# A twelfth pair: the last gate's second half of columns in seven products, and the final norm's products later

## The chip, the cores and the metric

The kernel runs on one core of one Trainium2 chip. The metric is the device time of one execution in microseconds (us), as the median of several runs. The profile and the trace come from one further execution, recorded by the hardware profiler. Engines are named as the profile names them: PE is TensorE (PEld its weight loads), DVE is VectorE, ACT is ScalarE, POOL is GpSimd, and SP issues most of the loads.

## The reference, cut to what matters

One layer of a hybrid decoder for 256 tokens of width 2048 in float32. The last two steps of it, and the norm behind them, are what the change touches:

```python
x = x + merged @ w_out
x = x + jax.nn.sigmoid(rmsnorm(x, ple_norm_g) @ w_pg) * (p_i @ w_pp)
return rmsnorm(x, final_norm_g)
```

`w_pg` is 2048 x 2048. Before that come one wide input projection (2048 x 13824), three branches (two kinds of attention and a gated recurrence), and their projections, which the change leaves alone.

## The kernel before, in words

**Products.** A float32 product is made of three matmuls: each operand is split into a high part of a shorter format (`fp32r`) and the rest, and `mm3` (lines 194 to 198) issues high x high, high x low and low x high into the same bank. Weights come as tiles of 128 x 1024: two k-tiles of 128 rows for 512 columns each (a chunk). `fetch` (line 112) loads one from SP's queue into one of six raw buffers; `split` casts the high part on ACT (line 141) and subtracts on DVE (line 147) into one of four pairs of buffers (`wsp`), or, for names in `kept`, into a block that stays. The 256 tokens are two halves of 128, and each half has its own bank of the matrix accumulators (`ps_mm`, two accumulators of two banks); four further banks (`ps_x`, the function `aux`) serve everything else.

**Pairs.** Two chunks of columns, a and b, can go together (`pair_of`, line 264). For the first four k-tiles (`PAIRED`) the work is seen as a 2 x 2 by 2 x 2 product: token halves by even and odd k-tiles, even and odd k-tiles by the two chunks. Eight block products become seven on sums and differences of the blocks. The activations' sums are made once (`make_sums`, line 248: five operations on DVE, a cast on ACT, a subtraction on DVE). The weights' sums are made in a chain tile: loads from SP, and adding loads from POOL's queue (`add_to`, line 275), each of which waits until the split before has read the tile. Products `seven`, `one`, `six` and `five` come ahead (`heads`) and leave partial results in two spare banks, which ACT and DVE move into the accumulators (`place`, line 281, and `on_vector`, line 277). Then `rest` runs the other twelve k-tiles of both chunks and sets `three`, `two` and `four` between them. Eleven pairs exist: nine in the input projection and two in the output projection.

**Order.** The program is traced as Python. A scheduler with a model of the engines then fixes each engine's order; `high_priority` moves an instruction ahead and `issue_after` ties one behind another. Every weight tile of `weights_of`, and some products of a pair, count as a tick (line 155): work given to `later(n, ...)` is put into the program n ticks on.

**The last stage.** The output projection's result is added to x (`residual`, line 1149), turned to feature-major through DRAM (`turn_later`, line 1066, on ACT's queue) and split into `x2T`. The gate (lines 1215 to 1259) has four chunks of 512 columns. Chunks 0 and 1 run their first twelve k-tiles each, then their last four; the last four need the part of x that is turned last. Chunk 2 follows whole. Chunk 3 is split for its end: first token half 0 with 512 columns, then token half 1 as two pieces of 256 columns, so that the final norm of the first half can run meanwhile; its weights stay in place (four blocks and the four split buffers). Behind each chunk, `output` (line 1181) makes the sigmoid on ACT, the product with the parked `p_i @ w_pp` (`pps`), the sum with x, and the squares for the final norm; the function that it returns multiplies by the final norm's weights `fg` (line 1188), and `gated` (line 1210) calls it at once. `pps` and `fg` are loaded on ACT's queue from two ticks after the output projection on (line 1174). At the end `store` scales by the norm and writes out.

Of the kernel before, what the change touches and what calls it, by code (L numbers as in the profile page):

```python
# [16 lines left out]
P = 128  # L17
D = 2048
SEQ = 256
NH = SEQ // P  # L20
BW = D // 2
KD = D // P
KB = BW // P
CW = 512
# [23 lines left out]
THEN = 2  # L48
SETTLE = 10
RV = 384  # L50
PAD = 256
# [3 lines left out]
def trunk(ctx: ExitStack, tc: tile.TileContext, x, early, table, onehot, maskv, w_in, sinks, conv, w_ri, vec, fin, w_br,  # L55
# [138 lines left out]
    def mm3(ps, a, b, first, last, **more):  # L194
        (ah, al), (bh, bl) = a, b
        nc.tensor.matmul(ps, ah, bh, start=first, stop=False, **more)  # L196
        nc.tensor.matmul(ps, ah, bl, start=False, stop=False, **more)  # L197
        nc.tensor.matmul(ps, al, bh, start=False, stop=last, **more)  # L198

# [63 lines left out]

    def pair_of(act, sums, src, row, name, inside=False, adds=4, early=1):
        names = ("11", "12", "22", "21")
# [28 lines left out]
        def product(n, a, r, dst, start=False, stop=False):  # L294
            w = split(f"{name}_m{n}", r, n == 1)
            for q in range(2):
                mm3(dst, a(q), [t[:, q * CW : (q + 1) * CW] for t in w], q == 0 and start, q == 1 and stop,
                    skip_group_check=True)

# [40 lines left out]
        def two():  # L340
            pss.append(matrix_psum(f"{name}_1"))
            for h in range(NH):
                place(pss[1][:, h], z[h])
            r = raw_of(3)
            with tc.issue_after(banks[1]):
                product(2, whole(1, 0), r, pss[1][:, 0])
                if adds < 4:
                    on_vector(chain, chain, r, ALU.add)

        def four():  # L350
            product(4, whole(1, 1), chain, pss[1][:, 1])
            tick()
# [5 lines left out]

        def rest(ends, done, at_turn=(0, 2, 4), then=None):
            while coming and coming[0] in heads:  # L360
# [14 lines left out]

            turns = [(i, k) for a, b in zip((PAIRED,) + ends, ends) for i in range(2) for k in range(a, b, WT // CW)]
            for n, (i, k) in enumerate(turns):
                head(len(turns) - n)
                usual(i, k)
                if n in at_turn:  # L380
                    (three, two, four)[at_turn.index(n)]()
                if k + WT // CW == KD:
                    done(i, pss[i])
                if then is not None and n == THEN:
                    then()

        t = block(f"b_{name}")
# [481 lines left out]

    def flip(dst, srcs, n, name, queue=nc.sync):  # L870

# [6 lines left out]
        for a in range(4):  # L878
            queue.dma_start(to[a], t[quad[a]].rearrange("i (b c) -> i b c", b=4))
        queue.dma_start(dst, d)  # L880

# [184 lines left out]
    def turn_later(u, n, src, name, gain=None, ticks=TURN_LATE):  # L1066
# [14 lines left out]
        later(ticks, finish)  # L1081
        if n == 0 and name == "m":
            later(ticks + 1, lambda: sums_of(u, name))

# [88 lines left out]
    for n, (to, src) in enumerate(rows):  # L1173
        later(2 + n, lambda to=to, src=src: nc.scalar.dma_start(to, src))
    HW = CW // 2
# [25 lines left out]
    def store(h, r, pieces):  # L1201
        for eng, c0, c1 in pieces:
# [5 lines left out]
            eng.dma_start(out[h * P : (h + 1) * P, c0:c1], sl)  # L1208

    def gated(n, ps):  # L1210
        y, junk = token_major(temp(f"y{n}")), token_major(temp(f"jz{n}"))
        for h in range(NH):
            output(h, n * CW, CW, ps[:, h, :], y[:, h, :], junk[:, h, :], square_act(h, n))()

    pss = [matrix_psum(f"pg{i}").rearrange("p h c -> p (h c)") for i in range(2)]
    gets = [weights_of(w_pg, i * KD * CW // WT, f"pg{i}", WT // CW) for i in range(2)]
    for last in (False, True):
        for i in range(2):
            for k in range(KD - 4, KD) if last else range(KD - 4):
                w, kk = gets[i](k)  # L1220
                c = slice(kk * CW, (kk + 1) * CW)
                for h in range(NH):
                    mm3(pss[i][:, h * CW : (h + 1) * CW], [t[:, h * P : (h + 1) * P] for t in act_of(*x2T)[k]],
                        [t[:, c] for t in w], k == 0, k == KD - 1)
            if last:
                gated(i, pss[i].rearrange("p (h c) -> p h c", h=NH))
    gated(2, project(act_of(*x2T), w_pg, 2 * KD * CW // WT, "pg2"))

    kept.update(f"pg3_{s}" for s in range(KD // 4))
# [6 lines left out]
    nc.gpsimd.tensor_tensor(rs3[:, :1], part[:, :1], half_c[:, :1], op=ALU.pow)  # L1236
    store(0, rs3[:, :1], ((nc.sync, 0, BW), (nc.scalar, BW + CW, D), (nc.sync, BW, BW + CW)))

    def part_of(c):
        def get(k):  # L1240
            w, kk = ws(k)
            return [t[:, kk * CW + c * HW : kk * CW + (c + 1) * HW] for t in w], 0
        return get
# [114 lines left out]
```

## Time and profile before

| what | us |
|---|---|
| median of 3 runs | 979.05 |
| lowest and highest of them | 978.0 and 981.14 |
| the profiled execution's own time | 977.16 |
| its span, first to last instruction | 975.1 |
| PE busy in the span | 965.5 |
| DVE busy | 721.8 |
| ACT busy | 620.9 |

The profiled execution is a little faster than the median, so a sum made on its rows is carried to the median by the difference. The granted clock of TensorE is 0.998. In the views, a line such as `L147 DVE TENSOR_TENSOR wl_pg<-r_pg,wh_pg` names the source line, the engine, the operation, and what is written from what. In order of time, the first number of a row is its start from the beginning of the span, the second its duration; in groups, busy time and the mean of one stand behind the bar; idle time ahead of an instruction and what ended it stand last.

### The profile page before, as it was taken

The page shows a single profiled execution, that of the slowest core. Times are in us where ns is not written, and L with a number is a line of the kernel's source. Part 1 is how long each engine was busy: PE and PEld are TensorE (multiplying, and loading weights), DVE is VectorE, ACT ScalarE, POOL GpSimd, SP SyncE. Part 2 cuts the span into 40 slices and gives each one's busy share as a digit, 9 for nine tenths or more (in the row PEclk, how much of TensorE's full clock was granted, in tenths as well). Part 3 has the DMA queues.
Part 4 walks back from the last instruction along what each step waited for, and adds up shares of the span by engine and source line. Part 5 has one row for each costly group of instructions (what it writes and reads, how often), then busy time and mean ns, then how long its engine had stood idle before and what let it go on. Part 6 is the DMA issues. An engine that isn't in the chain of part 4 may idle for free.

```text
span 975.1 us, 12612 instructions
## 1 busy us (share of the span) xinstructions
PE 965.5 (99%) x4390; PEld 804.3 (82%) x4390; DVE 721.8 (74%) x1005; ACT 620.9 (64%) x881; POOL 33.1 (3%) x45
## 2 busy tenths in 40 slices
PE   9999999999999999999999999999999999999996
PEld 7888888888888888888888888888888888888886
DVE  6855898866897676667677788788578587765673
ACT  7654776667777666556566866765566565665652
POOL 0010000010000000000000000000000000000000
PEclk9999999999999999999999999999999999999999
DMA  9978989799989865897787876776978998788742
GB/s 342 352 236 253 328 270 340 249 308 281 305 266 321 257 219 189 249 280 244 237 282 245 286 230 225 231 227 208 303 203 280 301 297 305 254 278 334 233 151 87
DMA packets 90264, 255.71 MB, mean 262 GB/s; under 512 B 10152, under 2 KB 31704, under 8 KB 90072
## 3 DMA queue, kind: packets, MB, share of 16 engines
q1 hardware_dynamic: 72720, 216.69, 64.4%
q0 software_dynamic: 4752, 17.30, 9.8%
q10 hardware_dynamic: 12728, 20.91, 6.4%
q8 instruction: 34, 0.56, 0.2%
q14 instruction: 30, 0.25, 0.1%
HBM read 234.13 MB, written 20.75 MB: 261 GB/s over the span
## 4 chain that ended last, share of the span: by engine, by line
PE 98%; DMA 0%; DVE 0%; ACT 0%; SPq 0%; issue 0%; DVEq 0%; ACTq 0%
PE ps_in L197 21%; PE ps_in L196 20%; PE ps_in L198 20%; PE ps_pg L198 3%; PE ps_pg L196 3%; PE ps_pg L197 3%; PE ps_out L196 3%; PE ps_out L198 3%; PE ps_out L197 3%; PE ps_bra L197 1%; PE ps_bra L196 1%; PE ps_brc L197 1%; PE ps_brc L198 1%; PE ps_brc L196 1%; PE ps_brb L197 1%; PE ps_brb L196 1%
## 5 line engine op out<-in xcount | busy, mean ns | idle before, releaser
L147 DVE TENSOR_TENSOR wl_in<-r_in,wh_in 128x1024 fp32r<-128x1024 f32 x196 | 239.0, 1222 | 95.6 <-ACT wh_in L141 91.3
L197 PE MATMUL ps_in<-wl_in,h 128*128 128x512 f32 x784 | 305.6, 390 | 0.4 <-DVE wl_in L147 0.4
L196 PE MATMUL ps_in<-wh_in,h 128*128 128x512 f32 x784 | 305.6, 390 | 0.0
L198 PE MATMUL ps_in<-wh_in,h 128*128 128x512 f32 x784 | 305.3, 389 | 0.0
L141 ACT CAST wh_in<-r_in 128x1024 fp32r<-128x1024 f32 x196 | 205.3, 1051 | 141.3 <-PE ps_in L198 105.1
L197 PEld LDWEIGHTS ps_in<-wl_in,h 128*128 128x128 f32 x784 | 147.3, 188 | 30.4 <-DVE wl_in L147 0.8
L198 PEld LDWEIGHTS ps_in<-wh_in,h 128*128 128x128 f32 x784 | 147.2, 188 | 30.4
L196 PEld LDWEIGHTS ps_in<-wh_in,h 128*128 128x128 f32 x784 | 147.2, 188 | 30.0
L147 DVE TENSOR_TENSOR wl_in_m<-b_in,wh_in_m 128x1024 fp32r<-128x1024 f32 x36 | 43.9, 1220 | 22.7 <-ACT wh_in_m L141 22.2
L147 DVE TENSOR_TENSOR wl_pg<-r_pg,wh_pg 128x1024 fp32r<-128x1024 f32 x28 | 33.9, 1222 | 27.4 <-ACT wh_pg L141 26.6
L141 ACT CAST wh_in_m<-b_in 128x1024 fp32r<-128x1024 f32 x36 | 37.8, 1049 | 25.0 <-PE ps_in L198 13.1
L275 POOL DMA_DIRECT2D b_in<-w_in_dram x29 | 25.5, 878 | 638.6 <-DMA b_in<-w_in_dram 395.7
L196 PE MATMUL ps_pg<-wh_pg,x_hi 128*128 128x512 f32 (+1 forms) x120 | 45.0, 375 | 0.0
L197 PE MATMUL ps_pg<-wl_pg,x_hi 128*128 128x512 f32 (+1 forms) x120 | 45.0, 375 | 0.0
L198 PE MATMUL ps_pg<-wh_pg,x_lo 128*128 128x512 f32 (+1 forms) x120 | 45.0, 375 | 0.0
L141 ACT CAST wh_pg<-r_pg 128x1024 fp32r<-128x1024 f32 x28 | 29.1, 1049 | 22.1 <-PE ps_pg L198 17.3
L196 PE MATMUL ps_out<-wh_out,m_hi 128*128 128x512 f32 x96 | 37.3, 389 | 0.0
L197 PE MATMUL ps_out<-wl_out,m_hi 128*128 128x512 f32 x96 | 37.3, 389 | 0.0
L198 PE MATMUL ps_out<-wh_out,m_lo 128*128 128x512 f32 x96 | 37.3, 389 | 0.0
L147 DVE TENSOR_TENSOR wl_out<-r_out,wh_out 128x1024 fp32r<-128x1024 f32 x24 | 29.1, 1220 | 10.2 <-ACT wh_out L141 10.2
L141 ACT CAST wh_out<-r_out 128x1024 fp32r<-128x1024 f32 x24 | 25.2, 1050 | 12.5 <-PE ps_out L198 8.1
L141 ACT CAST wh_brb<-r_brb 128x1024 fp32r<-128x1024 f32 x16 | 16.9, 1053 | 20.6 <-PE ps_brb L198 10.9
(360 smaller groups left out, 1638.3 us busy)
## 6 DMA issues: line engine op xcount, KB each, us to landing
r_in<-w_in_dram SPq DMA_DIRECT2D x223, 512.0 KB, 4.9
r_pg<-w_pg_dram SPq DMA_DIRECT2D x32, 512.0 KB, 4.8
r_out<-w_out_dram SPq DMA_DIRECT2D x30, 512.0 KB, 5.0
b_in<-w_in_dram POOLq DMA_DIRECT2D x29, 512.0 KB, 8.4
b_in<-w_in_dram SPq DMA_DIRECT2D x18, 512.0 KB, 5.3
r_brc<-w_br_dram SPq DMA_DIRECT2D x16, 512.0 KB, 6.3
r_bra<-w_br_dram SPq DMA_DIRECT2D x16, 512.0 KB, 4.3
r_brb<-w_br_dram SPq DMA_DIRECT2D x16, 512.0 KB, 6.3
```

Source lines behind the costliest of these rows:

```text
L141: casts.append(nc.scalar.copy(hi[:, c], r[:, c]).ins)
L147: los.append(nc.vector.tensor_tensor(lo[:, c], r[:, c], of, op=ALU.subtract).ins)
L196: nc.tensor.matmul(ps, ah, bh, start=first, stop=False, **more)
L197: nc.tensor.matmul(ps, ah, bl, start=False, stop=False, **more)
L198: nc.tensor.matmul(ps, al, bh, start=False, stop=last, **more)
L275: nc.gpsimd.dma_start(t, src[row + i], accum_op=ALU.add)
```

## The change

Chunks 2 and 3 of the gate become a pair (`parts=True`). Chunk 1's and chunk 0's products are interleaved with its `heads`: the pair is opened at chunk 0, k = 8; `seven` comes before chunk 1's k = 10, `one` and `six` before chunk 0's k = 12 and 14, `five` before chunk 1's k = 12. With `parts`, chunk 3's accumulator is not one of two banks but three tiles of the spare banks: token half 0 with 512 columns, and token half 1 as two pieces of 256, so that product `four` has twice the matmuls at half the width. `rest` then runs only chunk 2's own twelve k-tiles with `three`, `two` and `four` among them; chunk 3's own twelve k-tiles run behind, in the same three pieces as before, with a fixed order between the pieces. Of their six weight tiles two stay in blocks and four in the split buffers.

The sums of `x2T`'s first four k-tiles are made 12 ticks after these are there. The multiplication by `fg` of chunks 0 to 2 is collected in a list and issued, one operation for every second k-tile, among chunk 3's first piece. The loads of `pps` and `fg` start 10 ticks after the output projection instead of 2. The weights of chunks 2 and 3 are packed in the pair's order. `flip` gets an argument that nothing passes, and `READ` is not used.

```diff
+SUMS_LATE = 12
+PARKED_LATE = 10
+OPEN_AT = (0, 8)
...
         def product(n, a, r, dst, start=False, stop=False):
             w = split(f"{name}_m{n}", r, n == 1)
+            to = dst if type(dst) is list else [dst]
+            cw = CW // len(to)
             for q in range(2):
-                mm3(dst, a(q), [t[:, q * CW : (q + 1) * CW] for t in w], q == 0 and start, q == 1 and stop,
-                    skip_group_check=True)
+                for c, ps in enumerate(to):
+                    o = q * CW + c * cw
+                    mm3(ps, a(q), [t[:, o : o + cw] for t in w], q == 0 and start, q == 1 and stop, skip_group_check=True)
...
         def two():
+            if parts:
+                pss.append([aux(f"ps_{name}_{c}") for c in range(3)])
+                place(pss[1][0], z[0])
+                for c, t in enumerate(pss[1][1:]):
+                    place(t[:, :QW], z[1][:, c * QW : (c + 1) * QW])
...
         def four():
+            if parts:
+                product(4, whole(1, 1), chain, [t[:, :QW] for t in pss[1][1:]])
...
-            turns = [(i, k) for a, b in zip((PAIRED,) + ends, ends) for i in range(2) for k in range(a, b, WT // CW)]
+            turns = [(i, k) for a, b in zip((PAIRED,) + ends, ends) for i in chunks for k in range(a, b, WT // CW)]
...
-        if n == 0 and name == "m":
-            later(ticks + 1, lambda: sums_of(u, name))
+        if n == 0:
+            later(ticks + (1 if name == "m" else SUMS_LATE), lambda: sums_of(u, name))
...
-        later(2 + n, lambda to=to, src=src: nc.scalar.dma_start(to, src))
+        later(PARKED_LATE + n, lambda to=to, src=src: nc.scalar.dma_start(to, src))
...
+    weighing = []
+
     def gated(n, ps):
         y, junk = token_major(temp(f"y{n}")), token_major(temp(f"jz{n}"))
         for h in range(NH):
-            output(h, n * CW, CW, ps[:, h, :], y[:, h, :], junk[:, h, :], square_act(h, n))()
+            weighing.append(output(h, n * CW, CW, ps[:, h, :], y[:, h, :], junk[:, h, :], square_act(h, n)))
...
     for last in (False, True):
         for i in range(2):
             for k in range(KD - 4, KD) if last else range(KD - 4):
+                if (i, k) == OPEN_AT:
+                    open_pair, pair = pair_of(lambda: act_of(*x2T), lambda: sums["x2"], w_pg, row, "pg2", early=0, parts=True)
+                    open_pair()
+                if (i, k) in ((1, KD - 6), (0, KD - 4), (0, KD - 2), (1, KD - 4)):
+                    coming.pop(0)()
...
-    gated(2, project(act_of(*x2T), w_pg, 2 * KD * CW // WT, "pg2"))
-
-    kept.update(f"pg3_{s}" for s in range(KD // 4))
-    ws = weights_of(w_pg, 3 * KD * CW // WT, "pg3", WT // CW)
+    pss = pair((KD,), lambda i, ps: gated(2, ps), chunks=range(1))
+    row += PAIRED + (KD - PAIRED) * CW // WT
+    kept.update(f"pg3_{s}" for s in range(2))
+    ws = weights_of(w_pg, row, "pg3", WT // CW)
...
-    ps = project(act_of(*x2T), None, 0, "pg3", weights=ws, half=0)
-    output(0, c0, CW, ps, y[:, 0, :], junk[:, 0, :], square_act(0, 3))()
+    def last_products(at, h, c, n):
+        with tc.issue_after(ends[at - 1]) if at else nullcontext():
+            return products(at, h, c, n)
+
+    def products(at, h, c, n):
+        for k in range(KD - PAIRED):
+            w, kk = ws(k)
+            if weighing and n == CW and kk:
+                weighing.pop(0)()
+            ends[at] = mm3(pss[1][at][:, :n], [t[:, h * P : (h + 1) * P] for t in act_of(*x2T)[PAIRED + k]],
+                [t[:, kk * CW + c : kk * CW + c + n] for t in w], False, k == KD - PAIRED - 1, skip_group_check=True)
+        return pss[1][at][:, :n]
+
+    output(0, c0, CW, last_products(0, 0, 0, CW), y[:, 0, :], junk[:, 0, :], square_act(0, 3))()
...
     for c in range(2):
-        ps = project(act_of(*x2T), None, 0, f"pg{3 + c}", cw=HW, weights=part_of(c), half=1)[:, :HW]
+        ps = last_products(1 + c, 1, c * HW, HW)
...
-        "w_pg": _pack(a["w_pg"][0]),
+        "w_pg": np.concatenate([_pack(a["w_pg"][0][:, :BW]), _pack_pair(a["w_pg"][0][:, BW:])]),
```

More of the change, by code (lines that the diff above doesn't have):

```diff
@@ L49 @@
 SETTLE = 10
+SUMS_LATE = 12
+PARKED_LATE = 10
+READ = 3
+OPEN_AT = (0, 8)
 RV = 384
@@ L197, in mm3 @@
         nc.tensor.matmul(ps, ah, bl, start=False, stop=False, **more)
-        nc.tensor.matmul(ps, al, bh, start=False, stop=last, **more)
+        return nc.tensor.matmul(ps, al, bh, start=False, stop=last, **more).ins
     coming = []
@@ L262, in make_sums, with pair_of @@
         return parts
-    def pair_of(act, sums, src, row, name, inside=False, adds=4, early=1):
+    def pair_of(act, sums, src, row, name, inside=False, adds=4, early=1, parts=False):
         names = ("11", "12", "22", "21")
@@ L340, in two @@
         def two():
-            pss.append(matrix_psum(f"{name}_1"))
-            for h in range(NH):
-                place(pss[1][:, h], z[h])
+            if parts:
[3 more added lines that the diff above has]
+                    place(t[:, :QW], z[1][:, c * QW : (c + 1) * QW])
+            else:
+                pss.append(matrix_psum(f"{name}_1"))
+                for h in range(NH):
+                    place(pss[1][:, h], z[h])
             r = raw_of(3)
             with tc.issue_after(banks[1]):
-                product(2, whole(1, 0), r, pss[1][:, 0])
+                product(2, whole(1, 0), r, pss[1][0] if parts else pss[1][:, 0])
                 if adds < 4:
@@ L350, in four @@
         def four():
-            product(4, whole(1, 1), chain, pss[1][:, 1])
+            if parts:
+                product(4, whole(1, 1), chain, [t[:, :QW] for t in pss[1][1:]])
+            else:
+                product(4, whole(1, 1), chain, pss[1][:, 1])
             tick()
@@ L357, in pair_of, with rest @@
         heads = [seven, one, six, five] + [settle] * early
-        def rest(ends, done, at_turn=(0, 2, 4), then=None):
+        def rest(ends, done, at_turn=(0, 2, 4), then=None, chunks=range(2)):
             while coming and coming[0] in heads:
@@ L385, in rest @@
                     then()
+            return pss
         t = block(f"b_{name}")
@@ L868, in softmax_norm, with flip @@
                 nc.vector.tensor_scalar_mul(es[:, ks, j, :], es[:, ks, j, :], den[:, j, c : c + 1])
-    def flip(dst, srcs, n, name, queue=nc.sync):
+    def flip(dst, srcs, n, name, queue=nc.sync, ticks=0):
         t = temp(f"flip_{name}").rearrange("p k t -> p (k t)")[:, : n * P]
@@ L879, in flip @@
             queue.dma_start(to[a], t[quad[a]].rearrange("i (b c) -> i b c", b=4))
-        queue.dma_start(dst, d)
+        if ticks:
+            later(ticks, lambda: queue.dma_start(dst, d))
+        else:
+            queue.dma_start(dst, d)
     def flipped(t, n):
@@ L1212, in gated @@
         for h in range(NH):
-            output(h, n * CW, CW, ps[:, h, :], y[:, h, :], junk[:, h, :], square_act(h, n))()
+            weighing.append(output(h, n * CW, CW, ps[:, h, :], y[:, h, :], junk[:, h, :], square_act(h, n)))
     pss = [matrix_psum(f"pg{i}").rearrange("p h c -> p (h c)") for i in range(2)]
     gets = [weights_of(w_pg, i * KD * CW // WT, f"pg{i}", WT // CW) for i in range(2)]
+    row = 2 * KD * CW // WT
     for last in (False, True):
@@ L1226, in trunk @@
                 gated(i, pss[i].rearrange("p (h c) -> p h c", h=NH))
-    gated(2, project(act_of(*x2T), w_pg, 2 * KD * CW // WT, "pg2"))
-    kept.update(f"pg3_{s}" for s in range(KD // 4))
-    ws = weights_of(w_pg, 3 * KD * CW // WT, "pg3", WT // CW)
+    pss = pair((KD,), lambda i, ps: gated(2, ps), chunks=range(1))
+    row += PAIRED + (KD - PAIRED) * CW // WT
+    kept.update(f"pg3_{s}" for s in range(2))
+    ws = weights_of(w_pg, row, "pg3", WT // CW)
     y, junk = token_major(temp("y3")), token_major(temp("jz3"))
     c0 = 3 * CW
-    ps = project(act_of(*x2T), None, 0, "pg3", weights=ws, half=0)
-    output(0, c0, CW, ps, y[:, 0, :], junk[:, 0, :], square_act(0, 3))()
+    ends = {}
+    def last_products(at, h, c, n):
[10 more added lines that the diff above has]
+    output(0, c0, CW, last_products(0, 0, 0, CW), y[:, 0, :], junk[:, 0, :], square_act(0, 3))()
     mean(0)
@@ L1237, in trunk @@
     store(0, rs3[:, :1], ((nc.sync, 0, BW), (nc.scalar, BW + CW, D), (nc.sync, BW, BW + CW)))
[L1239 to L1243, printed above, removed]
     for c in range(2):
-        ps = project(act_of(*x2T), None, 0, f"pg{3 + c}", cw=HW, weights=part_of(c), half=1)[:, :HW]
+        ps = last_products(1 + c, 1, c * HW, HW)
         sl = slice(c * HW, (c + 1) * HW)
```

## The prediction

> **What bounds the kernel now.** I read the page's first part, then the chain that ended last, then who waited on TensorE.
>
> ```profile
> span 975.1 us, 12612 instructions
> PE 965.5 (99%) x4390; PEld 804.3 (82%) x4390; DVE 721.8 (74%) x1005; ACT 620.9 (64%) x881; POOL 33.1 (3%) x45
> ...
> PE 98%; DMA 0%; DVE 0%; ACT 0%; SPq 0%; issue 0%; DVEq 0%; ACTq 0%
> ...
> PE busy L489 <- PEq L1350: 0.8, 1, 0.8
> PE ps_in L197 <- DVE wl_in L147: 0.4, 1, 0.4
> PE ps_pp L538 <- ACT whi_pp L536: 0.4, 1, 0.4
> ```
>
> TensorE (PE) is busy from the first microseconds to the last product, and its three waits add up to 1.6 us. The eleven pairs that exist already run inside this stretch without a wait worth naming. So time can be won in two ways only: fewer or cheaper matmuls, or a shorter tail behind the last one. It can be lost by any new wait of PE. Next I read the gate's own stretch: its matmuls by shape, and the first and last of each width in order of time.
>
> ```profile
> L196 PE MATMUL ps_pg<-wh_pg,x_hi 128*128 128x512 f32 x104 | 40.5, 389 | 0.0
> ...
> L197 PE MATMUL ps_pg<-wk_pg,x_hi 128*128 128x256 f32 x16 | 4.5, 283 | 0.0
> ...
> L197 PE MATMUL ps_pg<-wl_pg,x_hi 128*128 128x256 f32 x16 | 4.5, 283 | 0.0
> ...
> L196 PE MATMUL ps_pg<-wk_pg,x_hi 128*128 128x512 f32 x8 | 3.1, 389 | 0.0
> ```
>
> ```profile
> 879.19 0.39 PE L196 MATMUL ps_pg<-wh_pg,x_hi 128*128 128x512 f32 x1
> ...
> 955.35 0.28 PE L196 MATMUL ps_pg<-wk_pg,x_hi 128*128 128x256 f32 x1
> ...
> 966.74 0.28 PE L198 MATMUL ps_pg<-wh_pg,x_lo 128*128 128x256 f32 x1
> ```
>
> Each of lines 196, 197 and 198 has 104 + 8 matmuls of 512 columns here, 336 in all, and 32 of 256 columns, 96 in all. The mean of 389 ns is no price: matmuls overlap. The price is the distance of starts: (955.35 - 879.19) / 336 = 0.2267 us for 512 columns, and (966.74 - 955.35) / 95 = 0.1199 us for 256.
>
> **The change part by part.** *Matmuls.* For the first four k-tiles of columns 1024 to 2047 the kernel now issues 24 matmuls of 512 for chunk 2, 12 of 512 for chunk 3's first token half, and 24 of 256 for its second half. The pair puts seven products there. Six of them (seven, one, six, five, three, two) have 2 x 3 matmuls of 512, which is 36. The seventh, `four`, goes to two banks of 256 columns and has 12 of 256. So 36 + 36 cancel, 24 of 256 become 12: 12 x 0.12 = **1.44 us less on PE**. Every other product of the gate stays, in another order.
>
> *Where PE meets the new work.* By 0.2267 us a matmul from 879.19: `seven` starts after 132 matmuls (909.1), `six` after 168 (917.3), `five` after 186 (921.4), chunk 2's own products after 216 (928.2). The last chunk's first token half now ends at 955.35 + 1.44 = 956.8, the last matmul's turn at 965.4 (was 966.86).
>
> *Vector and scalar work added.* 35 weight tiles are split instead of 32 (16 + 7 + 12). The operand sums of x2 and the evictions are new; the same helper did them for m, and the out pairs give the evictions.
>
> ```profile
> L147 DVE TENSOR_TENSOR wl_pg<-r_pg,wh_pg 128x1024 fp32r<-128x1024 f32 x28 | 33.9, 1222 | 27.4 <-ACT wh_pg L141 26.6 <-DMA d_x<-flip_x 0.8
> ...
> L251 DVE TENSOR_TENSOR whole_m<-m_hi,m_lo x1: 1219/1219/1219, 746.9 to 746.9; 128x1024 f32<-128x1024 f32 x1
> L255 DVE TENSOR_TENSOR sums_m<-whole_m x1: 419/419/419, 749.2 to 749.2; 128x256 f32<-128x256 f32 x1
> L261 DVE TENSOR_TENSOR sum_m<-sums_m,sum_m x1: 1225/1225/1225, 754.3 to 754.3; 128x1024 fp32r<-128x1024 f32 x1
> ...
> L286 ACT ACTIVATE z_out<-m_out x4: 598/598/600, 784.2 to 827.9; 128x512 f32<-128x512 f32 x4
> L279 DVE TENSOR_TENSOR z_out<-z_out,m_out x2: 680/681/682, 790.3 to 828.6; 128x512 f32<-128x512 f32 x2
> ...
> sum 90.00, PE 87.02 PEld 73.84 DVE 57.97 ACT 49.31 POOL 1.26; mean PE 9.67 PEld 8.20 DVE 6.44 ACT 5.48 POOL 0.14
> ```
>
> VectorE (DVE): 3 x 1.22 + (1.22 + 4 x 0.42 + 1.22) + 2 x 0.68 = 9.1 us. ScalarE (ACT): 3 x 1.05 (a cast of this size in the fence on loads below), one cast of the sums as long as another (1.05), and some seven evictions of at most 0.60: 8.4 us. The last row is the sum of nine windows of 10 us from 880 to 970: DVE has 32 us free there, ACT 41. I cost this work at nothing; PE's running matmuls hide it. If a split came late, its own 1.05 + 1.22 us would be exposed. The sums are due in the tick of chunk 0's k = 8, at about 889, and first read at 909: some 20 us for 5.2 us of work, interleaved with splits as m's were.
>
> *The weighing put off* (line 1188) is six operations of 0.69 us that move from behind each gate chunk to the last chunk's first products; nothing is added. The loads of pp and fg (six on ACT's queue, 881 to 892 in the next fence) come eight ticks, some 16 to 20 us, later, past the turning load of 895.60 on the same queue. pp is first read by VectorE after 921, fg later, so both keep over 8 us.
>
> *Loads.* SP issues 33 w_pg loads instead of 32 (two of them into the chain tiles), POOL issues four adding ones: 512 KB each, five more. PE is not waiting for loads anywhere here, so the volume costs nothing. What counts is one dependency: the chain tile for `six` is `seven`'s chain with one row added by a POOL load, which can start only when `seven`'s split has read it. Behind `six`'s cast on ACT stand the casts of the next weight tiles, and PE waits for those in turn.
>
> ```profile
> 881.01 0.83 ACTq L1174 DMA_DIRECT2D pp<-pp_d  x2
> ...
> 891.52 0.36 ACTq L1174 DMA_DIRECT2D fg<-fin_dram  x1
> ...
> 895.60 0.33 ACTq L880 DMA_DIRECT2D turn_x<-d_x  x1
> ...
> 903.17 1.71 ACT L1077 ACTIVATE turn_x<-turn_x,vecs 128x256 f32<-128x256 f32 x4 [3.69 <-DMA turn_x<-d_x]
> 904.78 1.03 ACT L141 CAST wh_pg<-r_pg 128x1024 fp32r<-128x1024 f32 x1
> 905.85 1.22 DVE L147 TENSOR_TENSOR wl_pg<-r_pg,wh_pg 128x1024 fp32r<-128x1024 f32 x1 [5.11 <-ACT wh_pg L141]
> ...
> 261.34 0.86 POOL L275 DMA_DIRECT2D b_in<-w_in_dram  x1 [17.18 <-DVE wl_in_m L147]
> ...
> 268.52 1.05 ACT L141 CAST wh_in_m<-b_in 128x1024 fp32r<-128x1024 f32 x1 [2.22 <-DMA b_in<-w_in_dram]
> 269.61 1.23 DVE L147 TENSOR_TENSOR wl_in_m<-b_in,wh_in_m 128x1024 fp32r<-128x1024 f32 x1 [0.60 <-ACT wh_in_m L141]
> ...
> b_in<-w_in_dram POOLq DMA_DIRECT2D x29, 512.0 KB, 8.4
> b_in<-w_in_dram SPq DMA_DIRECT2D x18, 512.0 KB, 5.3
> ...
> DMA to landing us min/median/max: 4.4/7.5/12.1
> ```
>
> `seven`'s split takes the place in the order that the cast at 904.78 has now. Its buffer is free at 901 (96 matmuls after 879.19), yet ACT stood 3.69 us for the turned x2, so the low part (the DVE row of 905.85) ended at 907.07. At worst the same holds after the change. The nearest row for the rest is the one add that a cast did wait for: 261.34 to 268.52 is 7.2 us; cast and low part then take 2.3 us (268.52 to 270.84). That gives 916.6, against 917.3 when PE reaches `six`: 0.7 us early. By the queue's median of 8.4 it would be 917.8 and PE would wait 0.5; by the slowest landing of this tile, 12.1, it would be 921.5 and PE would wait 4.2. From the other side, without ACT's stop, the split ends some 3.7 us sooner and all but the slowest landing fit. I take **0**: the six parked loads no longer share the engines with the turning load, which took 7.6 us there (issued 895.60, ACT went on at 903.17).
>
> The row says that an adding load lands 3.1 us after a plain one would (8.4 against 5.3). The Trainium skill, page "DMA: Bandwidth & Descriptors" (its table of first-byte latency), gives a load issued by GpSimd about 1 us to the first byte and one issued by SP or ACT about 0.6. An estimate by that page would put an add at 5.3 + 0.4 = 5.7 us, and `six` would have over 3 us in hand. The trace does not bear it out for the adding loads.
>
> *The tail.* Its code stays. In order of time it has these rows:
>
> ```profile
> 955.55 0.69 ACT L1184 ACTIVATE y<-ps_pg,rs 128x512 f32<-128x512 f32 x1 [3.80 <-PE ps_pg L198]
> ...
> 959.50 0.55 POOL L1236 TENSOR_TENSOR rs<-part,half_c 128x1 f32<-128x1 f32 x1 [69.61 <-DVE part L1199]
> ...
> 960.09 1.15 DVE L1205 TENSOR_SCALAR xr<-xr,rs 128x1024 f32<-128x1024 f32 x2 [0.66 <-POOL rs L1236]
> ...
> 960.09 0.72 ACT L1207 ACTIVATE xr<-xr,rs 128x512 f32<-128x512 f32 x1 [1.64 <-POOL rs L1236]
> 961.30 0.47 ACT L1184 ACTIVATE y<-ps_pg,rs 128x256 f32<-128x256 f32 x1 [0.49 <-PE ps_pg L198]
> ...
> 963.80 0.15 DVE L1199 TENSOR_SCALAR part<-part 128x1 f32<-128x1 f32 x1
> ...
> 967.06 0.47 ACT L1184 ACTIVATE y<-ps_pg,rs 128x256 f32<-128x256 f32 x1 [3.82 <-PE ps_pg L198]
> ```
>
> From the last sigmoid (967.06) to the end are 8.04 us. After the change the first token half's sigmoid starts at 957.0, its scale is ready near 961.5, its two DVE scalings run 961.5 to 962.7 and ACT's 961.5 to 962.3. The first quarter's sigmoid (ready at 961.3) then runs behind ACT's scaling at worst, 962.3 to 962.7, and its own chain (2.65 us from 961.30 to 963.95 now) ends at 965.1. The last sigmoid comes at 965.6. So a margin that is 3.1 us now shrinks to 0.5 us and still holds: 0 us. **Sum: -1.44 us.** The profiled execution took 977.16 us (span 975.1 and 2.06 around it), so 975.7 by its own time. The median of the runs, 979.05, lies 1.89 above that execution, which I carry over: **977.6**.
>
> **The rivals.**
> (a) *The add for `six` lands late by a little.* For it: 0.7 us of margin, and a median landing that eats it. Against: the order's freed loads, and 29 adding loads of the earlier pairs without a PE wait. At the median PE waits 0.5: 979.05 - 1.44 + 0.5 = 978.1.
> (b) *The tail's margin goes.* The six weighings are 6 x 0.69 = 4.1 us of DVE work; with gate chunk 2's four operations and one split (4 x 0.69 + 1.22) they make 8.1 us in the 8.2 us of the first token half's products. If four of them still stand before that half's own chain, it is 2.7 us later, DVE's scalings end at 965.4, ACT's at 965.0, and the first quarter's chain, now behind them, ends at 967.5. The last chain needs DVE from 966.1: 1.0 to 1.4 us lost, 978.0 + 0.6 = 978.6 or a little more. Against: fg is there and DVE idles half of the window 940 to 950 and can take the first four early:
>
> ```profile
> 940.00:950.00 10.00, 10.00 (x46) 8.29 (x45) 5.11 (x6) 3.55 (x5) 0.00 (x0) 1.00 0.00 1
> ```
>
> (c) *Slower.* The same place as (a), but ACT stops at the turned x2 as now and the add takes the slowest landing, 12.1: PE waits 4.2 us, 979.05 - 1.44 + 4.2 = 981.8. It is slower than before from a landing of 9.3 us on (907.07 + 9.3 + 2.3 = 917.3 + 1.44), and slower by more than runs can tell from 12.3 on. Against: it takes both at once.
> (d) *No saving:* the twelve missing matmuls stand in the last stage, which already feeds the tail; if the tail's vector work set the end, 979.05. The rows speak against it: ACT idles 3.82 us before the last sigmoid, waiting for PE.
>
> **How the numbers follow.** Forecast 0.67, (a) 0.10, (b) 0.09, (c) 0.06, (d) 0.04; 0.04 for what I do not see. A difference of 0.3%, 2.9 us, is about what can be told from no change; the runs shown lie from 1.05 below to 2.09 above their median. The forecast's -1.44 crosses -2.9 only if the runs add 1.5 of their own, about one time in six: 0.11, and with half of the unseen 0.13 for faster. Slower: (c), half of the unseen and some scatter of (d), 0.10. Same: 0.77. The range takes in (a), (b) and (d) and scatter of 2 us below the forecast: 975.6 to 980.4.
>
> **What would show it.** Right: 84 instead of 96 gate matmuls of 256 columns and 336 of 512, PE's last start near 965.3 counted from a gate that starts at 879.2, no PE wait in the gate, 8.0 us from the last sigmoid to the end, a span near 973.7. Wrong step by step: a PE wait at a product whose weights come from the chain tile, with ACT idle on a landing before it, is (a) or (c); the last sigmoid's DVE operations starting later than 0.5 us after it is (b); the first token half's scalings running past the last matmul is (b) too. The forecast fails if PE idles anywhere in the gate by more than 1.4 us, or if the order before 879 moves.

## The result and the profile after

| | before | after |
|---|---|---|
| median of 7 runs each, us | 978.54 | 987.76 |
| lowest and highest, us | 977.19 and 981.14 | 982.23 and 989.93 |
| the profiled execution: own time, span, us | 977.16, 975.1 | 987.76, 986.0 |
| granted clock of TensorE | 0.998 | 0.993 |

The changed kernel is slower: ratio 1.0082, interval 1.0057 to 1.0107. A ratio, here and below, is the recorded one over all runs and not the quotient of the two medians. One execution in run 1 below and one in run 6 ran at a much lower granted clock and are left out of the ratios. The forecast was 977.6, with 975.6 to 980.4 as its range, so the time lies outside.

The page of the kernel after: busy times, the chain that ended last, and the two lines of waits of PE that are new (us in total, times, longest).

```profile
span 986.0 us, 12630 instructions
...
PE 969.5 (98%) x4378; PEld 805.3 (82%) x4378; DVE 729.9 (74%) x1016; ACT 626.6 (64%) x892; POOL 36.7 (4%) x49
...
PE 92%; DMA 4%; DVE 1%; ACT 1%; issue 1%; ACTq 0%; SPq 0%; DVEq 0%
```

```profile
PE ps_pg L200 <- ACT wh_pg L145: 6.1, 2, 4.4
...
PE ps_pg L201 <- DVE wl_pg L151: 0.5, 1, 0.5
```

There are 12 matmuls fewer (4378 against 4390), as the change says, but PE's share of the chain fell from 98% to 92%, and transfers stand in it with 4%. Before, PE waited nowhere in the gate; now it waits 6.1 + 0.5 us there, in two places. In order of time (start, duration, operation, and in brackets the idle time before it and what ended it):

```profile
880.14 0.39 PE L200 MATMUL ps_pg<-wh_pg,x_hi 128*128 128x512 f32 x1
...
906.44 0.79 PE L200 MATMUL ps_pg<-wh_pg,x_hi 128*128 128x512 f32 x1 [4.39 <-ACT wh_pg L145]
907.70 0.79 PE L201 MATMUL ps_pg<-wl_pg,x_hi 128*128 128x512 f32 x1 [0.47 <-DVE wl_pg L151]
908.29 0.63 PE L202 MATMUL ps_pg<-wh_pg,x_lo 128*128 128x512 f32 x1
...
910.85 0.43 PE L202 MATMUL ps_pg<-wh_pg,x_lo 128*128 128x512 f32 x1
...
911.36 0.40 PE L201 MATMUL ps_pg<-wl_pg,x_hi 128*128 128x512 f32 x1
...
927.31 0.49 PE L200 MATMUL ps_pg<-wh_pg,x_hi 128*128 128x512 f32 x1 [1.73 <-ACT wh_pg L145]
...
931.55 0.39 PE L201 MATMUL ps_pg<-wl_pg,x_hi 128*128 128x512 f32 x1
```

Behind each wait the matmuls are slow for a while. From 908.29 to 910.85 are six starts of 512 columns, 0.427 us each; the usual distance is 0.2267. The clock column (the third from the end) of the view by stretches shows why. The clock was already at half before PE started again: it fell at 904.08, 2.0 us into the first wait, and stayed there until 910.91.

```profile
905.00:906.50 1.50, 0.06 (x1) 0.06 (x1) 0.08 (x1) 1.15 (x2) 0.00 (x0) 0.50 0.44 101
...
914.00:925.00 11.00, 11.00 (x51) 9.09 (x50) 4.94 (x5) 2.86 (x3) 0.91 (x1) 1.00 1.02 360
...
929.00:931.00 2.00, 2.00 (x6) 1.54 (x6) 1.75 (x2) 1.52 (x3) 0.00 (x0) 0.50 0.84 106
```

**The account.** The gate, from its first matmul to the last sigmoid's start, took 967.06 - 879.19 = 87.87 us before and 977.70 - 880.14 = 97.56 after (the sigmoid's row is in the next fence). The forecast was 87.87 - 1.44 = 86.43, so 11.13 us were lost: 4.39 + 0.47 + 1.73 = 6.59 of waiting; ten starts from 906.44 to 911.36 that take 4.92 - 0.47 = 4.45 us instead of 10 x 0.2267 = 2.27, so 2.18 of slower matmuls, most of it the half clock; ten more from 927.31 to 931.55, 4.24 instead of 2.27, so 1.97 (the clock fell 0.66 us behind their start). That is 10.74; 0.4 stays unnamed. Outside the gate little moved: it starts 0.95 us later, and from the last sigmoid to the end are 8.30 us against 8.04.

**What the first wait waits for.** Here are the instructions of ACT and of its queue:

```profile
889.19 1.15 ACTq L896 DMA_DIRECT2D d_x<-flip_x  x2
...
890.40 1.37 ACTq L896 DMA_DIRECT2D d_x<-flip_x  x2
...
904.88 0.34 ACTq L900 DMA_DIRECT2D turn_x<-d_x  x1
905.35 1.04 ACT L145 CAST wh_pg<-r_pg 128x1024 fp32r<-128x1024 f32 x1 [11.48 <-DMA r_pg<-w_pg_dram]
...
925.26 1.04 ACT L145 CAST wh_pg_m<-b_pg 128x1024 fp32r<-128x1024 f32 x1 [6.75 <-DMA fg<-fin_dram]
...
977.70 0.47 ACT L1204 ACTIVATE y<-ps_pg,rs 128x256 f32<-128x256 f32 x1 [1.45 <-PE ps_pg L202]
```

The turn of x through DRAM writes four pieces of 128 KB (`d_x`) on ACT's queue and loads the turned block behind them (`turn_x`). That load can be issued only when all four have landed, and ACT takes its work in order: the cast of 905.35 stands behind the issue. The name in the bracket, `r_pg`, is not what held it; the row above it is. The chain that ended last says the same:

```profile
891.27 13.52 DMA d_x<-flip_x
904.88 3.41 DMA turn_x<-d_x
```

Before, the same step ran so (the issue that follows, at 895.60, stands in the prediction):

```profile
887.82 0.81 ACTq L879 DMA_DIRECT2D d_x<-flip_x  x2
...
888.75 1.34 ACTq L879 DMA_DIRECT2D d_x<-flip_x  x2
```

From the end of the last issue, 890.09, to 895.60 are 5.5 us; after the change, from 891.77 to 904.88, 13.1. What is new beside these writes are POOL's adding loads:

```profile
887.58 0.89 POOL L279 DMA_DIRECT2D b_pg<-w_pg_dram  x1 [102.20 <-DMA b_pg<-w_pg_dram]
888.86 0.88 POOL L279 DMA_DIRECT2D b_pg<-w_pg_dram  x1 [0.39 <-issue]
...
915.85 0.91 POOL L279 DMA_DIRECT2D b_pg<-w_pg_dram  x1 [24.59 <-DVE wl_pg_m L151]
```

The two that open the pair go out at 887.58 and 888.86, just ahead of the four writes. The third is the add for `six`: issued at 915.85, its cast begins at 925.26, 9.4 us later. The cast of the next weight tile stands behind it on ACT, at 926.22, and PE meets that one as the second wait. The bracket of 925.26 names `fg`, and the chain that ended last a plain load of weights; that it is the add is shown by runs 1 to 3, where the bracket of the same cast is the add's own load, and by run 5. The last two numbers of the stretch from 890 to 900 are the transfer engines' share and GB/s; the first row is the kernel before, the second the one after:

```profile
890.00:900.00 10.00, 10.00 (x46) 8.29 (x45) 6.33 (x6) 5.16 (x5) 0.00 (x0) 1.00 1.03 408
```

```profile
890.00:900.00 10.00, 10.00 (x46) 8.29 (x45) 5.94 (x8) 3.05 (x3) 0.71 (x1) 1.00 1.02 270
```

The engines are full in both, but move a third less after the change. How the queues share them is in the view of transfers (packets, MB, share of the 16 engines' time; q0 holds POOL's adding loads, q1 SP's loads, q10 ACT's queue with the writes). First the kernel after from 895 to 898, then the kernel before from 891 to 893:

```profile
q0 software_dynamic: 96, 0.39, 65.4%
q1 hardware_dynamic: 95, 0.39, 34.2%
q10 hardware_dynamic: 93, 0.08, 7.7%
```

```profile
q10 hardware_dynamic: 424, 0.39, 55.9%
q1 hardware_dynamic: 116, 0.41, 50.1%
```

After the change the three queues get through equal numbers of packets. But a packet of an adding load is 4096 bytes and takes 0.327 us (median), one of a plain load takes 0.159 for the same bytes, and one of the writes is 1024 bytes and takes 0.046. So the writes pass 31 packets in a microsecond, where they passed 212 before, with one other queue at work. So the theory to be tested: *adding loads, though few, keep the transfer engines busy long enough to delay the small writes of the turn; and the add for `six` lands later than the 7.7 us that were at hand.* The rivals: the parked loads or the weighing, which were moved; the volume of the added loads, whatever their kind; the work added to DVE and ACT.

### The profile page after: what moved, and what is told of

Same layout as the page of the kernel before. It is cut to its first block, busy times and chain, and to the rows that moved or that the text cites. A ratio compares the mean times of both kernels' runs of the same rounds, so it can differ in the third digit from the quotient of the medians.

```text
span 986.0 us, 12630 instructions
## 1 busy us (share of the span) xinstructions
PE 969.5 (98%) x4378; PEld 805.3 (82%) x4378; DVE 729.9 (74%) x1016; ACT 626.6 (64%) x892; POOL 36.7 (4%) x49
## 4 chain that ended last, share of the span: by engine, by line
PE 92%; DMA 4%; DVE 1%; ACT 1%; issue 1%; ACTq 0%; SPq 0%; DVEq 0%
PE ps_in L201 20%; PE ps_in L200 20%; PE ps_in L202 20%; PE ps_out L200 2%; PE ps_out L201 2%; PE ps_out L202 2%; DMA d_x<-flip_x 2%; PE ps_pg L200 2%; PE ps_pg L201 2%; PE ps_pg L202 2%; PE ps_bra L200 1%; PE ps_bra L201 1%; PE ps_brc L201 1%; PE ps_brc L200 1%; PE ps_brc L202 1%; PE ps_brb L201 1%
## 5 line engine op out<-in xcount | busy, mean ns | idle before, releaser
L151 DVE TENSOR_TENSOR wl_pg<-r_pg,wh_pg 128x1024 fp32r<-128x1024 f32 x26 | 31.6, 1222 | 27.2 <-ACT wh_pg L145 27.2
L200 PE MATMUL ps_pg<-wh_pg,x_hi 128*128 128x512 f32 (+1 forms) x112 | 43.0, 384 | 6.1 <-ACT wh_pg L145 6.1
L145 ACT CAST wh_pg<-r_pg 128x1024 fp32r<-128x1024 f32 x26 | 27.0, 1048 | 29.1 <-DMA r_pg<-w_pg_dram 11.5
L201 PE MATMUL ps_pg<-wl_pg,x_hi 128*128 128x512 f32 (+1 forms) x112 | 43.0, 384 | 0.5 <-DVE wl_pg L151 0.5
L202 PE MATMUL ps_pg<-wh_pg,x_lo 128*128 128x512 f32 (+1 forms) x112 | 42.7, 381 | 0.0
L151 DVE TENSOR_TENSOR wl_out<-r_out,wh_out 128x1024 fp32r<-128x1024 f32 x24 | 29.1, 1220 | 11.5 <-ACT wh_out L145 11.1
L200 PEld LDWEIGHTS ps_pg<-wh_pg,x_hi 128*128 128x128 f32 x112 | 21.7, 193 | 10.8 <-ACT wh_pg L145 7.0
```

Source lines behind the costliest of these rows:

```text
L145: casts.append(nc.scalar.copy(hi[:, c], r[:, c]).ins)
L151: los.append(nc.vector.tensor_tensor(lo[:, c], r[:, c], of, op=ALU.subtract).ins)
L202: return nc.tensor.matmul(ps, al, bh, start=False, stop=last, **more).ins
```

## The experiments

Each ratio is against the kernel before, in runs of the same chip.

**1. The pair opened earlier.** The two opening adding loads are moved ahead of chunk 0's first k-tile.

```diff
-OPEN_AT = (0, 8)
+OPEN_AT = (0, 0)
```

> The changed kernel, with the pair opened at the gate's first weight tile (chunk 0, k = 0) instead of k = 8, so that the chain tiles' four loads go out some 10 us sooner, ahead of the turn of x2's last part. Theory A (the two adding loads of the opening meet the turn's small writes on the DMA engines, ACT stands for the turn 11 us and PE starves): the writes land in about 6 us again, the first PE wait of 4.9 us and the half clock behind it go; what remains is the wait for the add before `six` (1.7 us and its own half clock), so about 978 to 981. Theory B (the turn is late from the volume of loads in the gate's start, whenever the pair opens): the first wait stays, 986 to 988.

Median 986.44, ratio 1.0068 (1.0048 to 1.0088). The time hardly came back, and it is the one that was expected of the rival, volume. The trace has the reason: the adds now meet another turn. In order of time:

```profile
870.10 0.87 POOL L279 DMA_DIRECT2D b_pg<-w_pg_dram  x1 [0.88 <-DMA b_pg<-w_pg_dram]
...
871.93 1.05 ACTq L896 DMA_DIRECT2D d_x<-flip_x  x2
...
885.77 0.34 ACTq L900 DMA_DIRECT2D turn_x<-d_x  x1
886.21 2.94 ACT L145 CAST wh_pg<-r_pg 128x1024 fp32r<-128x1024 f32 x3 [10.43 <-DMA d_x<-flip_x]
```

The third turn's writes wait 12.8 us (872.98 to 885.77), ACT stands 10.43 us, PE waits 1.74 + 0.76 us at 887. The last turn, which now has no adds beside it, delays nothing; the add for `six` still costs 1.45 us at 927.5. The first wait moved with the loads that are held to make it.

**2. The same, with the parked loads kept away from the adds.** The first two go out early, the rest much later.

```diff
-        later(PARKED_LATE + n, lambda to=to, src=src: nc.scalar.dma_start(to, src))
+        later((2 + n) if n < 2 else 15 + n, lambda to=to, src=src: nc.scalar.dma_start(to, src))
```

> As the run before, and the parked loads parted: the two loads of pp that the first chunk needs at ticks 2 and 3, the other pp loads and fg from tick 17 on, behind the add before `six`. Theory A with its second half (the late parked loads meet the add before `six`, which took 9.3 us): no PE wait in the gate at all, 977 (the 1.44 us of the twelve matmuls saved). Theory B: 984 to 988. If the parked loads did not slow the add: the same time as the run before.

984.14, ratio 1.0048 (1.0028 to 1.0067). The opening still costs 1.83 + 0.76 us at 884. The add for `six` is issued at 913.15 and its cast starts at 922.53, 9.4 us as before, and PE waits 1.51 us. So the late parked loads are not what makes this add slow; that half of the theory fell.

**3. The opening's two adds on VectorE.** Two more plain loads and two DVE additions in the place of two adding loads; the adds of `six` and of the next chain step stay.

```diff
-                add_to(t, i)
+                if not parts:
+                    add_to(t, i)
+        if parts:
+            for t, i in ((chain, 2), (lone, 0)):
+                key = f"{name}_first_{i}"
+                fetch(src, row + i, key)
+                on_vector(t, t, raws.pop(key)[0], ALU.add)
```

> The changed kernel with the pair opened where it is (k = 8), but the two adds of the opening made on DVE: two plain loads more on SP's queue and two additions of 1.22 us, no adding load there; the adds before `six` and `four` stay. The same bytes are loaded at the same place. Theory A (it is the adding loads): the turn lands in time, first wait gone, 978 to 982. Theory B (it is the volume): the first wait stays, 985 to 988.

983.96, ratio 1.0046 (1.0026 to 1.0067). The issue of the turn's writes ends at 891.5 and the load goes out at 897.21, after 5.7 us, with the same bytes loaded beside them. The first wait is gone; a new one of 0.70 us stands at 891.85, for a low part behind the two additions on DVE. The wait for the add of `six` is longer:

```profile
922.01 0.50 PE L200 MATMUL ps_pg<-wh_pg,x_hi 128*128 128x512 f32 x1 [2.85 <-ACT wh_pg L145]
```

The add for `six` took from 910.14 to 919.96, 9.8 us, and PE now comes earlier to it. So there are two causes, and mending one hands part of the gain to the other; the time is above the 978 to 982 that were expected.

**4. Only the parked loads and the weighing.** The kernel before, with the loads of pp and fg from the tenth tick on and the multiplication by fg put off; no pair.

```diff
+PARKED_LATE = 10
...
-        later(2 + n, lambda to=to, src=src: nc.scalar.dma_start(to, src))
+        later(PARKED_LATE + n, lambda to=to, src=src: nc.scalar.dma_start(to, src))
...
-            output(h, n * CW, CW, ps[:, h, :], y[:, h, :], junk[:, h, :], square_act(h, n))()
+            weighing.append(output(h, n * CW, CW, ps[:, h, :], y[:, h, :], junk[:, h, :], square_act(h, n)))
...
+    ps = project(act_of(*x2T), None, 0, "pg3", weights=ws, half=0, hooks={k: weigh_one for k in range(5, KD, 2)})
```

> The kernel before with the second part of the change alone: parked loads 10 ticks on, the final norm's products of three chunks put off to chunk 3's first piece; no pair. Theories A and B: nothing of it meets the turn, no PE wait, 978.5, the same as before within 0.2%. Theory C (the second part costs by itself, by the parked loads on ACT's queue or by DVE's work near the end): at least 2 us more than before.

980.16, ratio 1.0021 (1.0003 to 1.0039): not nothing, but about a quarter of the loss. In its profile PE waits 0.94 + 0.76 us at 903, at a cast that stands behind the turned x2 in ACT's order (ACT idles 3.90 us for it at 900.28).

**5. The later adds on VectorE.** The opening's two adding loads stay, the two behind them become DVE additions.

```diff
-                    open_pair, pair = pair_of(lambda: act_of(*x2T), lambda: sums["x2"], w_pg, row, "pg2", early=0, parts=True)
+                    open_pair, pair = pair_of(lambda: act_of(*x2T), lambda: sums["x2"], w_pg, row, "pg2", adds=2, early=0, parts=True)
```

> The changed kernel with the pair's two later additions (into the chain tile before `six` and before `four`) on DVE, as the output projection's pairs have them, and the opening's two adding loads left where they are. Theory A (two separate collisions: the opening's adding loads delay the turn, and the add before `six` lands 9 to 11 us after its issue where 7.7 us are at hand): the first PE wait stays (3 to 5 us and half clock behind it), the second near `six` goes; 982 to 985. Theory D (the second wait only follows from the first, since ACT is late from then on): the second wait stays without the adding load.

983.63, ratio 1.0052 (1.0037 to 1.0068). The mirror of run 3: the second wait is gone, the first stays, 3.45 + 0.47 us at 906.75, with the turn's load issued at 905.20 and half clock for 6.83 us.

**6. No adding load at all.** Runs 3 and 5 together.

> All four additions of the pair on DVE: no adding load in the gate. Theory A: neither wait, at most a wait under 1 us from the two additions on DVE near 891; 977 to 979, that is 0 to 1.4 us below the kernel before. Theory E (the turned x2 is waited for in the changed order of ACT whatever the loads are): a wait of 1 us or more near 903 to 910 stays, 980 or more.

977.93, ratio 0.9990 (0.9978 to 1.0003). The whole loss is gone. The trace that is read here is of a second set of executions of this kernel:

> The kernel without adding loads in the gate once more, for a profile of it and a closer ratio. Theory A: no PE wait in the gate above 1 us, no half clock, the turn's writes land within 6 us of the last issue; 0.997 to 1.000 of the kernel before. If a wait stays, the missing part of the 1.44 us is there.

978.53, ratio 0.9993 (0.9984 to 1.0002). One wait is left in the gate, 1.01 us at 893.16, for a low part that stands behind the two new additions on DVE. The gate takes 968.66 - 880.88 = 87.78 us.

**7. The pair opened between two turns,** with the later adds on VectorE (run 5 with the opening at chunk 0's k = 4).

> As the first of this series (later additions on DVE), and the pair opened at chunk 0, k = 4: the two adding loads should fall between the turning writes of x2's third and fourth part (869 to 876 and 889 to 895). Theory A: the loads land by 890, no wait above 0.5 us, 977 to 978.5. If the loads still meet the writes, the wait is at 887 or at 905 as in the runs before, 980 to 985.

984.67, ratio 1.0056 (1.0035 to 1.0076). The plan missed: the adds went out at 889.89 and 891.17 all the same, since SP's loads into the chain tiles stand behind weight loads that wait for a raw buffer, and met the same turn. PE waited 3.02 + 0.76 us at 908. Moving a line in the program did not move the transfer.

**8. Four loads more, and nothing else.** The kernel before, with two plain loads and two adding loads at the opening's place into a block that nothing reads; all products are those of before.

```diff
+                if not last and (i, k) == (0, 8):
+                    t = block("b_pg")
+                    with tc.issue_after(loads[-1]):
+                        for c, n in ((0, 18), (WT, 16)):
+                            nc.sync.dma_start(t[:, c : c + WT], w_pg[17])
+                            nc.gpsimd.dma_start(t[:, c : c + WT], w_pg[n], accum_op=ALU.add)
```

> The kernel before with nothing of the change but four loads: at chunk 0, k = 8, two plain and two adding loads of 512 KB into a block that nothing reads. Theory A: the turn's last four writes land 10 us or more after their issue (5.5 us in the kernel before); what PE loses depends on the casts that stand ahead of the turn on ACT, 0 to 5 us, 979 to 984. Theory B or C: the turn lands as before, 978.5.

985.80, ratio 1.0072 (1.0056 to 1.0088) for four loads whose data nobody uses. The time is above the 979 to 984 that were expected, and it comes about in another way. The adding loads go out at 896.20 and 897.88, behind the writes, which took no longer than before (5.0 us from the end of their last issue, 895.87, to the load's issue). What they delay is the turn's load, and a load of weights beside it, the second row here, which the chain that ended last goes through:

```profile
900.85 0.33 ACTq L880 DMA_DIRECT2D turn_x<-d_x  x1
...
901.19 13.03 DMA r_pg<-w_pg_dram
...
915.27 1.70 ACT L1077 ACTIVATE turn_x<-turn_x,vecs 128x256 f32<-128x256 f32 x4
```

The turn's load has 14.4 us from issue to use, where the kernel before had 7.6 (895.60 to 903.17). It landed after 12.7; the rest is the weight tile's cast at 914.31, which stands ahead in ACT's order. PE waits 2.44 us at 918.90 and 1.27 us in three shorter waits. The gate took 92.76 us, 4.89 more than before. It also started 2.9 us later, before any of the four loads; one trace doesn't say whether that belongs to the kernel.

**9. The same four loads, all plain.** The only edit to run 8 is `accum_op`.

```diff
-                            nc.gpsimd.dma_start(t[:, c : c + WT], w_pg[n], accum_op=ALU.add)
+                            nc.gpsimd.dma_start(t[:, c : c + WT], w_pg[n])
```

> The control to the four loads put into the kernel before: the same four, from the same queues and at the same place, but the two of POOL's queue overwrite instead of add. Theory A (it is the adding): within 0.3% of the kernel before, 978 to 981. Theory B (volume and place): 984 to 987 as with the adding loads.

981.03, ratio 1.0030 (1.0017 to 1.0042). Same queue, bytes and place in the program (the two go out at 894.32 and 896.23, some 2 us earlier): 0.30% in the place of 0.72%, and the two intervals do not meet. In the gate's own time the difference is clearer: 88.17 us, 0.30 more than before, against 4.89. The turn's load takes 9.9 us to its use (900.72 to 910.59). The queues in the window 893 to 913 (packets, MB, share of the 16 engines' time; in the issue lines KB and median us to landing), first with adding loads, then with plain ones:

```profile
DMA packets 2356, 7.01 MB, mean 350 GB/s; under 512 B 264, under 2 KB 776, under 8 KB 2355
...
q0 software_dynamic: 288, 1.05, 26.9%
...
b_pg<-w_pg_dram POOLq DMA_DIRECT2D x2, 512.0 KB, 10.4
...
turn_x<-d_x ACTq DMA_DIRECT2D x1, 512.0 KB, 12.7
```

```profile
DMA packets 2678, 8.12 MB, mean 406 GB/s; under 512 B 314, under 2 KB 826, under 8 KB 2677
...
q0 software_dynamic: 288, 1.05, 13.0%
...
b_pg<-w_pg_dram POOLq DMA_DIRECT2D x2, 512.0 KB, 7.6
...
turn_x<-d_x ACTq DMA_DIRECT2D x1, 512.0 KB, 8.5
```

The same 1.05 MB in 288 packets take 26.9% of the engines' time when they add and 13.0% when they don't: twice as much, while the engines are full in both. (By packets of 4096 bytes, again 0.327 and 0.159 us.) Everything else in the window gets less.

**10. No adding loads, parked loads at their old ticks.** Run 6 with `PARKED_LATE = 2`.

> The same with the parked loads back at ticks 2 to 7, so only their place differs. If the late parked loads cost anything once the adding loads are gone (they change where ACT's order has the turn), this is faster than the run before it, up to 0.997; if they help, it is slower, with the turn waiting behind 3 MB of loads, 1.000 to 1.003.

978.21, ratio 0.9993 (0.9984 to 1.0002), so neither of the two expected outcomes. The only run of the pair without any wait of PE in the gate; these are its longest waits of PE in the whole execution, then the gate's first matmul and the last sigmoid:

```profile
PE busy L512 <- PEq L1393: 0.8, 1, 0.8
PE ps_in L200 <- ACT wh_in L145: 0.6, 2, 0.4
```

```profile
881.85 0.39 PE L200 MATMUL ps_pg<-wh_pg,x_hi 128*128 128x512 f32 x1
...
911.77 0.39 PE L200 MATMUL m_pg<-wh_pg_m,sum_x 128*128 128x512 f32 x1
...
920.15 0.39 PE L200 MATMUL m_pg<-wh_pg_m,sum_x 128*128 128x512 f32 x1
```

```profile
968.32 0.47 ACT L1210 ACTIVATE y<-ps_pg,rs 128x256 f32<-128x256 f32 x1 [1.45 <-PE ps_pg L202]
```

The gate takes 968.32 - 881.85 = 86.47 us: 1.40 less than before, where the sum said 1.44.

**What it comes to.** One trace of each kernel; the gate runs from its first matmul to the last sigmoid's start:

| kernel | gate starts, us | gate takes, us | PE waits in it, us |
|---|---|---|---|
| before | 879.19 | 87.87 | none |
| after | 880.14 | 97.56 | 6.59 |
| run 1, opened earlier | 882.69 | 93.64 | 3.95 |
| run 2, parked loads apart | 879.41 | 93.95 | 4.33 |
| run 3, opening's adds on DVE | 879.88 | 92.56 | 3.55 |
| run 4, no pair | 880.11 | 90.12 | 1.70 |
| run 5, later adds on DVE | 881.38 | 93.54 | 3.92 |
| run 6, no adding load | 880.88 | 87.78 | 1.01 |
| run 7, opened between turns | 883.40 | 92.40 | 3.78 |
| run 8, four loads, two adding | 882.06 | 92.76 | 3.71 |
| run 9, four plain loads | 881.97 | 88.17 | none |
| run 10, no adding load, parked early | 881.85 | 86.47 | none |

Shown: without adding loads the loss is gone (runs 6 and 10); adding loads alone cost 0.72%, and 4.9 us in the gate, half of what the change lost there (8); plain loads in their place cost 0.30%, and 0.3 us in the gate (9); the opening and the later adds are two separate waits (3, 5); each wait of the opening follows the turn that the adds meet (1); the small writes of the turn pass packet by packet in turn with the adding ones, and take 13.1 us beside them and 5.7 beside plain loads of the same bytes (3). Open: why the runs' times differ by more than their gates. In run 9 the median is 2.5 us above and the gate 0.3; in run 10 the 1.40 us that the gate saves don't show in the ratio, 0.9993. The gate's start varies from 879.19 to 883.40 in the table, by more than the saving; run 10's trace reached the output projection's first product at 802.7 us instead of 800.3, before anything of the change runs. The interval, from 0.9984, still holds the 0.9985 that the saving would give. No version here beats the kernel before by more than can be told.

## Why the prediction was wrong

**The step that failed first** is the sentence on loads: "PE is not waiting for loads anywhere here, so the volume costs nothing. What counts is one dependency", the add for `six`. That PE waits for no load says nothing of who else does. ACT waited for `turn_x`, 3.69 us in a row that the prediction itself quotes, and the writes of that turn were on the same 16 engines, which were full already (a share of 1.03 from 890 to 900). The opening's two adding loads were counted among five loads more and given no place in time. They stand at 887.58 and 888.86, against writes at 889.19: 4.86 us of waiting and 2.18 of slow matmuls behind it, 7.0 of the 11.1 us. It was no rival either. What an adding load takes of the engines could have been read beforehand, on the page of the kernel before (q0 has adding loads alone):

```profile
q1 hardware_dynamic: 72720, 216.69, 64.4%
q0 software_dynamic: 4752, 17.30, 9.8%
```

That is 1.9 times the engines' time for each MB.

**The second is a size.** "I take 0" for the add of `six` rested on a landing of 7.2 us, with 0.7 us to spare, and on parked loads "no longer sharing the engines with the turning load". The landing was 9.4 us here and 9.4 to 11.0 in runs 1 to 3 (issue of the add to the start of its cast). The parked loads have no part in it (run 2). Rival (c), "slower from a landing of 9.3 us on", had the mechanism for this wait, and its threshold was met; it was given 0.06 because it was thought to take the slowest landing of all. The queue's own median, 8.4 us, was on the page and above the row that was taken: the range of this tile's landings, 4.4 to 12.1, should have carried the chance. By the same sum a landing of 9.4 us makes PE wait 1.5 (907.07 + 9.4 + 2.3 - 917.3), and 1.73 was measured; the 1.97 of slow matmuls behind it was not in any sum.

**The third is a cost that no step has:** the clock after an idle TensorE. Every rival was priced as its wait alone. Here 6.59 us of waiting cost 10.74.

**What held.** The 1.44 us of fewer matmuls: 1.40 in run 10. The place of the products: `seven` and `six` were put 29.9 and 38.1 us behind the gate's start; in run 10 they come after 29.92 and 38.30. The work of DVE and ACT "at nothing": it is all there in run 10, which waits nowhere. The sums of x2, too: in run 10 the last of them ends at 908.7, 3 us before its product. The tail: the last store is issued 3.96 us after the last sigmoid's start in run 10 as in the kernel before, so the margin of 0.5 us was enough; from there to the end it took 0.3 to 0.4 us longer (after the change, runs 6 and 10). That run's trace speaks against rivals (b) and (d). The parked loads were nearly right: "both keep over 8 us" is true, but put off together with the weighing, without the pair, they cost 0.2% (run 4), through the turn that ACT meets in its order, which was the step's own subject in the fence on loads.

**The estimate by the Trainium skill** on first-byte latency ("DMA: Bandwidth & Descriptors", section "Specifications") would have made `six` safer still. (By the prediction's own sum, 907.07 + 5.7 + 2.3 against 917.3, that leaves 2.2 us in hand and not "over 3".) The runs go the other way: plain loads from POOL's queue landed in 7.6 us and adding ones in 10.4 at the same place, so the addition, not the issuing queue's start, is the larger part of an add's delay.

## What to carry to other kernels

Before a transfer is costed at nothing because the main engine waits for none, look for every engine that does wait for one in the same stretch, and for what stands in order behind that wait; small writes on which a load hangs suffered most here. Count an adding load as two plain ones in engine time and place it in time against such chains, by the trace of its issue and not by its line in the program. And where PE may idle for a few microseconds, price the slower clock with the wait.

## What the runs showed of the hardware

*An adding load.* 1.05 MB from POOL's queue took 26.9% of 20 us of the sixteen engines as adding loads and 13.0% as plain ones, 2.07 times as much (runs 8 and 9); by packets of 4096 bytes it is 0.327 against 0.159 us. The Trainium skill, "DMA: Bandwidth & Descriptors", section "Queues, rings and completion order", says that each engine goes round the queues that have work, a packet at a time. The trace agrees, in the packets that the profile counts: 96, 95 and 93 of three queues in 3 us. With the adding packets slow, the other queues have fewer turns: 7.01 MB moved with them and 8.12 without, the engines full both times.

*The clock.* Around the waits of 4.39 + 0.47 us the granted clock was 0.5 for 6.8 us, around one of 1.73 for 3.4 us, and the 0.427 us from start to start are 1.88 times the usual 0.2267. But a wait of 2.44 us in run 8 left the clock at 1.00, and so did one of 1.51 in run 2. The Trainium skill, "TensorE: Matmul & The Clock Gate", section "What's actually happening", puts this down to a window of about 3.4 us that runs freely. The traces agree: within each execution the clock's changes lie whole multiples of 3.413 us apart (after the change 904.08, 910.91, 927.97 and 931.39). Cut into windows on this grid, from 20 us on, every full-clock window with PE idle for 51% of it or more was followed by half clock, and none with 48% or less was. An edge at 918.08 divides run 8's wait, one at 923.75 run 2's, so that neither fills half a window. The Trainium skill's table there asks for an idle window of about 3.4 us; half of one was enough here, as in the wait of 1.73 us.
